# v of quarters 2 to 4 of a gMLP layer by seven half-size block products, with combined weights made beforehand

## The chip, the cores and the metric

The kernel runs on one core of a Trainium2 chip. The metric is the device time of one execution in microseconds (us). Engines are called as in the profile: PE (TensorE matmul), PEld (its weight load), DVE (VectorE), ACT (ScalarE), POOL (GpSimd) and SP (the engine that issues the DMAs here).

## The reference, cut to what matters

A trunk of two layers over 2048 tokens of width 1024, all in float32. Layer A is a chunked gMLP: it projects the normed and modulated input h to u, v and z (2048 columns each), mixes v over the tokens of a chunk of 128, and multiplies:

```
h = rms_norm(x, norm_g) * (1 + scale) + shift
u, v, z = jnp.split(h @ w_in, 3, axis=-1)
u = jax.nn.gelu(u)
v = rms_norm(jax.nn.gelu(v), sgu_g)
...
mixed = jnp.einsum('gts,bcsge->bctge', w_causal, v) + b_s.T[None, None, :, :, None]
y = u * mixed.reshape(bsz, s, A_WIDTH) * jax.nn.silu(z)
return x + gate * (y @ w_out)
```

Layer B projects keys and values once (`w_kv`), projects q (24 heads of 128) and a gate z from a second norm, and attends in three groups of heads: group 0 over neighbouring tokens, group 1 with dilation 4, group 2 with dilation 16. The three outputs are weighted by their softmax sums, gated and projected.

## The kernel before

**Precision.** Every float32 operand of a large product is split into a high part and a rest (`split`, L244: ACT copies the high part to the fp32r type, DVE subtracts it, L247). A product is then three matmuls of 128x512: high by high, high by low, low by high (`mm3`, L273).

**Quarters.** The work goes over the tokens in four quarters of 512 (Q = 0 to 3 in the code, quarters 1 to 4 here). In each quarter `layer_A` (L700) computes v (four blocks of 512 columns, `dense`, L277), then u and z (eight blocks each, `dense_f`, L299), then the output product (pd_o, `dense` again). `proj_B` (L793) follows with the key and value blocks (pd_kv), three q blocks (groups 2, 1, 0) and the gate block z (pd_z0b to pd_z3b). The last part, `finish` (L1105), makes the output of layer B.

`dense` loads 8 weight units of 128x512 for a block of columns, and runs them over the four token tiles in two pairs; one quarter's v is 4 x 8 x 4 x 3 = 384 matmuls and 32 weight units. The evacuation of v (`v_evac`, L559) is a Gelu from PSUM into the tile m and a square with its sum; m has two tiles of 128x4x1024. Then m is scaled (L711), and `mix` (L714) multiplies it with the chunk weights during u.

**Seven products.** The q and z blocks of layer B use `dense_s` (L376): a block of 512 tokens x 1024 x 1024 is cut into halves in each direction, and seven half-size products replace eight. Each is 4 k x 2 token tiles x 3 = 24 matmuls and 4 weight units. They go on two pairs of PSUM tiles, x and y; DVE adds partial results (`add`, L400). This needs sums of operands (`make_ops`, L491, names s1 to s4) and four combined weights t1 to t4 per block, which are made once: `combine_weights` (L320) loads the quarters of the weights, makes four subtractions of 128x512 on POOL (L344 to L347), and stores them to a DRAM tensor wt. It does so for four blocks in the first quarter, with `xin` tiles and `st` tiles in turn. The operands lie in four "big" tiles in the order 11, 12, 22, s1, s2, s3, s4 (`new_ops`, L460); "big" has six buffers of 16 KB per partition, and m takes two that these leave.

**Beside the stream.** Work for other engines and small pieces for PE are written as generators ("fillers"). `tick` (L84) is called after every few matmuls and runs `rate[0]` x its part steps of them. In quarter 1 the fillers are the modulation vectors and the combined weights; in layer A of quarters 2 to 4 they are the attention of the quarter before (`attend_local`, L1058: 80 steps, in quarter 3 with 8 more steps of `ada_gate`, each with two DVE instructions on L175 or L177); during the last blocks of `proj_B` they are the input of the next quarter (`make_hA`, L534: norm, transposes on PE, high part on ACT, low part on POOL, L456). What is left when `layer_A` returns is run at once (`drain`). The rate in layer A of quarters 2 to 4 is 1.5, so 24 steps fall into v, 24 into u, 24 into z and the rest into the output product. An attention step has its keys and values in an `xin` tile (`att_kv`, L906), makes scores on PE (L969 to L975), adds the bias on DVE (L978), takes exponentials on ACT (L988) and, in the form with `wrap`, three products and a select on POOL (L996 to L999, L1023).

**What sets the order.** Each engine has one queue and takes its instructions in order. That order is made by a planner before the run: it goes through the program with estimated durations and gives each engine, among the instructions that it takes for ready, the one that the program issues first. Buffers come from pools in turn (weights "w": 8 units, "raw" loads: 6, "xin": 4, "st" sum tiles: 8, "big": 6), and a tile waits until the last use of its buffer is over. `tc.issue_after` puts instructions behind a given one on its engine. All DMAs of the kernel are issued by SP.

Line 1260 and what follows is the loop over the quarters; `side_work` (L1245) is what quarter 1 has in the fillers.

## Time and profile before

| | us |
|---|---|
| median of 3 runs | 3000.92 (2997.74 to 3002.16) |
| the profiled execution, first to last instruction | 2998.7 |
| PE busy in it | 2951.4 |
| v of quarters 2, 3, 4 | 104.48, 106.04, 113.21 |
| output product of quarter 1 | 88.96 |
| one q block of quarter 2 | 38.08 |

The lengths of stages are the distances between the first matmuls of neighbouring stages in the trace, on the pd_ tiles of their names. The busy time of an engine in a stretch is the time in which at least one of its instructions runs; the mean of a group of matmuls is the time of one, and neighbours overlap. Idle time of an engine that is not the bottleneck costs nothing.

### The profile page before, as it was taken

To read this page: it belongs to the slowest core of one execution; us is meant where nothing else is said; L and a number is where in the kernel's file an instruction comes from. 1 tells how busy PE (TensorE), PEld (TensorE's weight loads), DVE (VectorE), ACT (ScalarE), POOL (GpSimd) and SP (SyncE) were. 2 spreads that over 40 slices of the span, in tenths; PEclk is the share of its full clock that TensorE was granted. 3 is DMA by queue.
4 is the path that set the end of the run, shared out by engine and by line. 5 is a ranking of instruction groups with operands and counts; after the bars stand their busy time and mean duration, and the time that the engine had idled before them with its cause. 6 is when DMAs were issued, how large, how long until landed. Compare 5 with 4: busy or idle time off the path is not lost.

```text
span 2998.7 us, 45113 instructions
## 1 busy us (share of the span) xinstructions
PE 2951.4 (98%) x14896; PEld 2473.5 (82%) x14896; DVE 1990.4 (66%) x3594; ACT 1625.1 (54%) x3308; POOL 744.4 (25%) x1044
## 2 busy tenths in 40 slices
PE   7999999999999999999999999999999999999999
PEld 5888888888888888888888888888888888977887
DVE  6868466764467376856567576856576576878772
ACT  4323355667366265756365366665465457866540
POOL 1057002410023013513123114323132020122322
PEclk9999999999999999999999999999999999999999
DMA  8899456763433366853433466833333366788642
GB/s 279 281 305 345 156 161 196 250 207 122 143 107 102 118 198 211 271 187 117 134 104 108 129 201 223 278 109 119 125 112 102 120 215 203 229 281 282 222 165 91
DMA packets 343677, 547.80 MB, mean 183 GB/s; under 512 B 36266, under 2 KB 135820, under 8 KB 343444
## 3 DMA queue, kind: packets, MB, share of 16 engines
q1 hardware_dynamic: 343444, 544.93, 56.4%
q8 instruction: 118, 1.93, 0.3%
q14 instruction: 115, 0.94, 0.1%
HBM read 439.28 MB, written 105.52 MB: 182 GB/s over the span
## 4 chain that ended last, share of the span: by engine, by line
PE 88%; DVE 3%; DMA 3%; issue 3%; POOL 2%; ACT 1%; SPq 0%; POOLq 0%; DVEq 0%; ACTq 0%
PE pd_o L275 11%; PE pd_v L275 10%; PE pd_kv L275 7%; PE pd_z L315 4%; PE pd_z L313 4%; PE pd_z L314 4%; PE pd_u L313 4%; PE po L1049 4%; PE pd_u L315 4%; PE pd_u L314 4%; PE pm L718 2%; PE pq L937 1%; PE pf L1227 1%; PE pf L1229 1%; PE pf L1228 1%
## 5 line engine op out<-in xcount | busy, mean ns | idle before, releaser
L275 PE MATMUL pd_o<-w_o,yh 128*128 128x512 f32 x1024 | 318.2, 391 | 0.0
L275 PE MATMUL pd_v<-w_v,hAh 128*128 128x512 f32 x960 | 303.5, 397 | 0.0
L275 PE MATMUL pd_kv<-w_kv,hkh 128*128 128x512 f32 x768 | 239.2, 393 | 0.3
L275 PEld LDWEIGHTS pd_o<-w_o,yh 128*128 128x128 f32 x1024 | 191.0, 188 | 39.1
L988 ACT ACTIVATE pr<-pr,stat,rt 128x256 f32<-128x256 f32 (+1 forms) x320 | 177.5, 556 | 62.7 <-DVE stat L982 36.8
L275 PEld LDWEIGHTS pd_v<-w_v,hAh 128*128 128x128 f32 x960 | 175.0, 188 | 37.8 <-issue 3.5
L313 PE MATMUL pd_u<-hAh,w_u 128*128 128x512 f32 x512 | 205.9, 402 | 0.0
L313 PE MATMUL pd_z<-hAh,w_z 128*128 128x512 f32 x512 | 204.6, 400 | 0.0
L315 PE MATMUL pd_z<-hAh,w_z 128*128 128x512 f32 x512 | 200.5, 392 | 0.0
L315 PE MATMUL pd_u<-hAh,w_u 128*128 128x512 f32 x512 | 200.2, 391 | 0.0
L275 PE MATMUL pd_o<-w_o,yl 128*128 128x512 f32 x512 | 200.0, 391 | 0.0
L314 PE MATMUL pd_z<-hAl,w_z 128*128 128x512 f32 x512 | 199.7, 390 | 0.0
L314 PE MATMUL pd_u<-hAl,w_u 128*128 128x512 f32 x512 | 199.7, 390 | 0.0
L275 PE MATMUL pd_v<-w_v,hAl 128*128 128x512 f32 x480 | 188.3, 392 | 0.0
L246 ACT ACTIVATE w_o<-raw_o 128x512 fp32r<-128x512 f32 x128 | 80.0, 630 | 184.6 <-PE pd_o L275 122.4
L246 ACT ACTIVATE w_u<-raw_u 128x512 fp32r<-128x512 f32 x128 | 78.7, 630 | 174.7 <-PE pd_u L315 78.3
L275 PEld LDWEIGHTS pd_kv<-w_kv,hkh 128*128 128x128 f32 x768 | 143.2, 189 | 30.6 <-ACT hkh L482 2.0
L247 DVE TENSOR_TENSOR w_o<-raw_o,w_o 128x512 fp32r<-128x512 f32 x128 | 91.9, 722 | 111.9 <-ACT w_o L246 111.4
L246 ACT ACTIVATE w_z<-raw_z 128x512 fp32r<-128x512 f32 x128 | 78.2, 627 | 160.9 <-PE pd_z L315 57.2
L996 POOL TENSOR_TENSOR dg<-pr,ident 128x256 f32<-128x256 f32 x76 | 60.5, 797 | 380.9 <-ACT pr L988 366.2
L1049 PEld LDWEIGHTS po<-kv,pT 128*128 128x128 f32 x1200 | 147.4, 192 | 8.5 <-ACT pT L899 2.1
L978 DVE SCALAR_TENSOR_TENSOR pr<-dist,rt,ps 128x256 f32<-128x256 f32 (+1 forms) x320 | 122.8, 431 | 43.0 <-PE ps L975 29.0
(664 smaller groups left out, 7680.8 us busy)
## 6 DMA issues: line engine op xcount, KB each, us to landing
raw_q<-in_b_w_in_dram SPq DMA_DIRECT2D x144, 256.0 KB, 3.4
raw_u<-in_a_w_in_dram SPq DMA_DIRECT2D x128, 256.0 KB, 3.6
raw_z<-in_a_w_in_dram SPq DMA_DIRECT2D x128, 256.0 KB, 3.2
raw_o<-in_a_w_out_dram SPq DMA_DIRECT2D x128, 256.0 KB, 3.0
raw_v<-in_a_w_in_dram SPq DMA_DIRECT2D x120, 256.0 KB, 4.1
qt<-qd SPq DMA_DIRECT2D x96, 260.0 KB, 2.9
raw_kv<-in_w_kv_dram SPq DMA_DIRECT2D x96, 256.0 KB, 2.9
od<-ot SPq DMA_DIRECT2D x96, 256.0 KB, 3.2
```

Source lines behind the costliest of these rows:

```text
L246: nc.scalar.activation(hi, src, AF.Copy)
L247: nc.vector.tensor_tensor(lo, src, hi.bitcast(F32), ALU.subtract)
L275: last_mm[0] = nc.tensor.matmul(pt, a, u[:, w, :], start=f, stop=e, skip_group_check=more)
L313: nc.tensor.matmul(pts[i], wh, hh[:, k, :], start=k == 0, stop=False)
L314: nc.tensor.matmul(pts[i], wh, hl[:, k, :], start=False, stop=False)
L315: nc.tensor.matmul(pts[i], wl, hh[:, k, :], start=False, stop=k == KT - 1)
L718: nc.tensor.matmul(pm[:, t * P:(t + 1) * P], m[e // 8][:, t, (e % 8) * P:(e % 8 + 1) * P], wst[:, e // 2, :], start=True, stop=True)
L937: nc.tensor.transpose(pq[:, h * P:(h + 1) * P], u["qt"][:, h * P:(h + 1) * P], ident)
L978: nc.vector.scalar_tensor_tensor(pr[:, i, :], dist[:, 256 - w:256], u["rt"][:, h:h + 1], psc[:, i, :], ALU.mult, ALU.add)
L988: nc.scalar.activation(pr[:, i, :], pr[:, i, :], AF.Exp, bias=mneg[:, i:i + 1], scale=u["rt"][:, h:h + 1], accum_out=lsum[:, i:i + 1])
L996: nc.gpsimd.tensor_tensor(dg, prev, ident.unsqueeze(1).broadcast_to([P, hp, P]), ALU.mult)
L1049: nc.tensor.matmul(po[:, h * P:(h + 1) * P], u["pT"][h // hp][:, h % hp, j, :], u["kv"][:, j, kh, 1, :], start=j == 0, stop=j == nk - 1)
```

## The change

Seven things are changed.

1. v of quarters 2 to 4 goes through `dense_s` in two blocks of 1024 columns (b = 4, 5), 2 x 7 x 24 = 336 matmuls and 56 weight units; quarter 1 keeps `dense`.
2. `sums_A` makes the operands out of hA: POOL adds high and low part into m[1] (four additions of 128x1024), DVE makes s1 to s4 in place, and each is split into two more big tiles. The DVE and ACT part is issued after the first product of the first block.
3. In the first of the two blocks `dense_s` has an order of its own (`late`): 11, 12 x 21, 22 x t4, then s2, s3, s1, s4, with 12 adds on DVE and 4 copies on ACT. The second block has the order that q and z have: 11, s2, 12, s3, s1, 22, s4, with 10 adds and 2 copies.
4. In these blocks the low half of every fourth weight unit is made by POOL (`shared`).
5. The combined weights of the two blocks are made in the output product of quarter 1, with `st` tiles alone, at rate 2.2 (before: rate 0).
6. Attention runs at rate 1.0 in v and 1.5 after it (1.6 in quarter 3): 16 steps in v, 24 in u, 24 in z, the rest in the output product. There its keys and values take a "w" buffer.
7. The operands of layer B lie in the order 11, 12, s2, s3, 22, s1, s4.

```diff
-    def split(hi, lo, src):
+    def split(hi, lo, src, e=None):
         nc.scalar.activation(hi, src, AF.Copy)
-        nc.vector.tensor_tensor(lo, src, hi.bitcast(F32), ALU.subtract)
+        (e or nc.vector).tensor_tensor(lo, src, hi.bitcast(F32), ALU.subtract)
...
-            split(u[:, 0, :], u[:, 1, :], raw)
+            split(u[:, 0, :], u[:, 1, :], raw, nc.gpsimd if shared and kk == nk - 1 else None)
...
+    def block_of(b):
+        return (b_w_in, b * D) if b < 4 else (a_w_in, AW + (b - 4) * D)
+
+    def combine_weights(blocks, where):
...
-                if i % 2:
+                if where == "sums" or where == "both" and i % 2:
...
+        if late:
+            product(x, "11", "11", True)
+            u2 = tmp("u")
+            for i in range(2):
+                nc.scalar.activation(u2[i][:, 0:512], x[i], AF.Copy)
+            late()
+            product(x, "12", "21", False)
+            for i in range(2):
+                evac(i, x[i], 0)
+            product(y, "22", "t4", True)
+            c21 = tmp("w")
+            for i in range(2):
+                nc.scalar.activation(c21[i][:, 0:512], y[i], AF.Copy)
+            product(x, "s2", "t2", True)
+            add(u2, x, u2)
+            product(y, "s3", "t3", True)
+            u3 = tmp("v")
+            add(u3, y, u2)
+            add(c21, [t[:, 0:512] for t in u3], c21)
+            for i in range(2):
+                evac(i + 2, c21[i], 0)
+            product(x, "s1", "t1", True)
+            add(u3, x, u3)
+            for i in range(2):
+                evac(i + 2, u3[i], 1)
+            add(u2, x, u2)
+            product(y, "s4", "22", True)
+            add(u2, y, u2)
+            for i in range(2):
+                evac(i, u2[i], 1)
+            return
...
-                for i, n in enumerate(("11", "12", "22", "s1", "s2", "s3", "s4"))}
+                for i, n in enumerate(("11", "12", "s2", "s3", "22", "s1", "s4"))}
...
+    def sums_A(Q, hA, m):
...
+        for n in ("11", "21", "22", "12"):
+            k, c = part[n]
+            hi, lo = (h[:, k:k + 4, c:c + 256].bitcast(F32) for h in hA)
+            nc.gpsimd.tensor_tensor(f[n], hi, lo, ALU.add)
+        s = {"s1": f["22"], "s3": f["21"], "s2": f["11"], "s4": f["12"]}
+
+        def sums():
+            nc.vector.tensor_tensor(s["s1"], f["21"], f["22"], ALU.add)
+            nc.vector.tensor_tensor(s["s3"], f["11"], f["21"], ALU.subtract)
+            nc.vector.tensor_tensor(s["s2"], s["s1"], f["11"], ALU.subtract)
+            nc.vector.tensor_tensor(s["s4"], f["12"], s["s2"], ALU.subtract)
+            for n in ("s2", "s3", "s1", "s4"):
+                split(*ops[n], s[n])
+        return ops, sums
...
     def layer_A(Q, hA, m, sqv, j0):
-        for j in range(j0, 4):
+        if Q:
+            ops, sums = sums_A(Q, hA, m)
+            for b in range(2):
+                ev = [v_evac(Q, m, sqv, 2 * b + n) for n in range(2)]
+                dense_s(ops, 4 + b, f"v{Q}{b}", lambda t, src, n: ev[n](t, src[:, 0:512]), None if b else sums, True)
+            rate[0] = 1.6 if Q == 2 else 1.5
+        for j in range(j0, 0 if Q else 4):
...
+        aside[0] = True
         if Q == 0:
-            rate[0] = 0
+            fillers.append(combine_weights((4, 5), "sums"))
+            rate[0] = 2.2
...
-        kv = xp.tile([P, 2, 512], F32, tag="xin", name=f"kv{g}_{b}")
+        pool, tag = (wp, "w") if aside[0] else (xp, "xin")
+        kv = pool.tile([P, 2, 512], F32, tag=tag, name=f"kv{g}_{b}")
...
-            rate[0] = 1.5
+            rate[0] = 1.0
         hk, hb, keep, rest = layer_A(Q, hA, m, sqv, 1 if Q == 0 else 0)
```

More of the change, by code (lines that the diff above doesn't have):

```diff
@@ L65, in trunk @@
     gd = dp.tile([2, D], F32, name="gd")
-    wt = [[dp.tile([512, 512], F32, name=f"wt{b}_{i}") for i in range(4)] for b in range(4)]
+    wt = [[dp.tile([512, 512], F32, name=f"wt{b}_{i}") for i in range(4)] for b in range(6)]
     fillers = []
@@ L318, in dense_f @@
             evac(i, pts[i])
-    def combine_weights():
-        todo = [(b, k) for b in (2, 1, 0, 3) for k in range(4)]
+    def block_of(b):
+        return (b_w_in, b * D) if b < 4 else (a_w_in, AW + (b - 4) * D)
+    def combine_weights(blocks, where):
+        todo = [(b, k) for b in blocks for k in range(4)]
         quads = {}
@@ L374, in sum_tile, with dense_s @@
         return tp.tile([P, 520], F32, tag="st", name=f"st_{nm}")
-    def dense_s(ops, b, nm, evac):
+    def dense_s(ops, b, nm, evac, late=None, shared=False):
         x, y = ([pst(f"pd_{nm}{c}{i}", "d") for i in range(2)] for c in "ab")
@@ L382, in dense_s @@
         flip[0] = not flip[0]
-        n0 = b * D
-        src = {"11": (b_w_in, 0, n0), "21": (b_w_in, 4, n0), "22": (b_w_in, 4, n0 + 512)}
+        w, n0 = block_of(b)
+        src = {"11": (w, 0, n0), "21": (w, 4, n0), "22": (w, 4, n0 + 512)}
         src.update({f"t{i + 1}": (wt[b][i], 0, 0) for i in range(4)})
         def product(pts, a, w, first):
-            us = wunits(*src[w], f"{nm}{w}_", 4)
+            us = wunits(*src[w], f"{nm}{w}_", 4, shared=shared)
             store_late(5)
@@ L557, in make_hA @@
                 yield
+    def sums_A(Q, hA, m):
+        t = [big.tile([P, 2, 2, 4, 256], F32R, tag="big", name=f"sA{Q}{i}") for i in range(2)]
+        ops = {n: (t[i // 2][:, i % 2, 0], t[i // 2][:, i % 2, 1]) for i, n in enumerate(("s2", "s3", "s1", "s4"))}
+        part = {"11": (0, 0), "12": (4, 0), "21": (0, 256), "22": (4, 256)}
+        f = {}
+        for i, (n, (k, c)) in enumerate(part.items()):
+            hi, lo = (h[:, k:k + 4, c:c + 256] for h in hA)
+            if n != "21":
+                ops[n] = hi, lo
+            f[n] = m[1][:, i, :].rearrange("p (k t) -> p k t", k=4)
+        for n in ("11", "21", "22", "12"):
[11 more added lines that the diff above has]
+        return ops, sums
     def v_evac(Q, m, sqv, j):
@@ L1246, in side_work @@
         yield from delayed(rest_of_ada())
-        yield from combine_weights()
+        yield from combine_weights((2, 1, 0, 3), "both")
     hA, m, sqv, ends = begin(affa)
@@ L1262, in trunk @@
             drain()
+        aside[0] = False
         nxt = {}
```

10 lines of the change are left out of this document (6 added, 4 removed).

## The prediction

> **What bounds the kernel now.** I read the page's span and busy lines first, then the chain of work that ended last, then the groups of matmuls, then one piece of the chain and the busy time by stage. Columns of a group: how many, total us, mean ns.
>
> ```profile
> span 2998.7 us, 45113 instructions
> PE 2951.4 (98%) x14896; PEld 2473.5 (82%) x14896; DVE 1990.4 (66%) x3594; ACT 1625.1 (54%) x3308; POOL 744.4 (25%) x1044
> ...
> PE 88%; DVE 3%; DMA 3%; issue 3%; POOL 2%; ACT 1%; SPq 0%; POOLq 0%; DVEq 0%; ACTq 0%
> ...
> L275 PE MATMUL pd_v<-w_v,hAh 128*128 128x512 f32 x960 | 303.5, 397 | 0.0
> L275 PE MATMUL pd_v<-w_v,hAl 128*128 128x512 f32 x480 | 188.3, 392 | 0.0
> ```
>
> TensorE is busy 98% of the span and is 88% of the chain, so a matmul that goes is worth its place in the stream. The mean of 397 ns is not that place: matmuls overlap. The chain in a q block, which already uses seven products, gives it:
>
> ```profile
> 1102.43 5.44 PE pd_q12a L275 x24
> 1107.87 5.44 PE pd_q12b L275 x24
> ...
> 1135.07 5.44 PE pd_q12a L275 x24
> 1140.51 0.68 PE pd_kv L275 x3
> ```
>
> Seven products of 24 matmuls take 1140.51 - 1102.43 = 38.08 us without a gap: 226.7 ns a matmul. Now the stages that matter (columns: stretch, length, then busy us and count of PE, PEld, DVE, ACT, POOL, granted clock, DMA share, GB/s). In order: z and output of quarter 1, v of quarter 2, a q block and the z block of quarter 2, v of quarters 3 and 4, a q block of quarter 4 with attention beside it.
>
> ```profile
> 234.43:321.56 87.13, 87.13 (x387) 72.18 (x386) 62.25 (x60) 37.95 (x65) 49.19 (x32) 1.00 0.99 336
> 321.56:410.52 88.96, 88.96 (x402) 73.68 (x401) 39.62 (x65) 27.36 (x53) 2.40 (x4) 1.00 0.37 114
> 634.89:739.37 104.48, 104.48 (x533) 87.90 (x532) 41.99 (x92) 71.16 (x150) 1.50 (x4) 1.00 0.38 122
> 1102.27:1140.35 38.08, 38.08 (x170) 31.54 (x168) 28.24 (x47) 23.85 (x41) 12.51 (x26) 1.00 0.70 205
> 1239.24:1280.24 41.00, 41.00 (x193) 33.89 (x192) 36.57 (x54) 27.44 (x46) 17.20 (x22) 1.00 0.88 289
> 1280.24:1386.28 106.04, 106.04 (x529) 87.66 (x528) 62.23 (x117) 60.31 (x126) 23.17 (x34) 1.00 0.48 154
> 1943.63:2056.84 113.21, 113.21 (x606) 96.49 (x605) 60.00 (x124) 71.68 (x149) 32.25 (x50) 1.00 0.36 117
> 2508.63:2601.48 92.85, 91.49 (x633) 82.09 (x632) 77.27 (x200) 79.21 (x229) 12.11 (x28) 1.00 0.74 226
> ```
>
> PE is full in all three v stages at clock 1.00. Vector and scalar engine have room there: 42 to 62 us and 60 to 72 us of 104 to 113. Everything below asks whether that room is enough.
>
> **What goes.** v of one quarter is 4 token tiles x 8 k x 4 blocks x 3 = 384 matmuls (1440 in the two groups = 288 in quarter 1 + 3 x 384). By seven products it is 2 x 168 = 336. So 3 x 48 = 144 matmuls go: 144 x 226.7 ns = **-32.6 us**. Nothing is added on PE. The attention steps are only placed elsewhere: 16 instead of 24 of them beside v, 8 more beside the output stage, where DVE is at 39.62 of 88.96.
>
> **How long the new v stage is on PE.** Attention takes what is left of a stage after 384 x 0.2267 = 87.1 us: 17.4, 19.0 and 26.1 us for 24 steps. With 16 steps it is about 11.6 in quarter 2 and 17.4 in quarter 4; in quarter 3 eight of the 16 are gate steps, so about 9.5. With 336 x 0.2267 = 76.2: 87.8, 85.7 and 93.6 us.
>
> **What the other engines must do in that time.** The prices (DVE splits by stretch, then groups of quarter 2, of quarter 3, of quarter 4 and of the whole run):
>
> ```profile
> 234.43:321.56 87.13, 32.86 (x33) 1.00 0.99 336
> 634.89:739.37 104.48, 21.21 (x33) 1.00 0.38 122
> 1102.27:1140.35 38.08, 18.86 (x29) 1.00 0.70 205
> 1280.24:1386.28 106.04, 22.86 (x33) 1.00 0.48 154
> 1943.63:2056.84 113.21, 20.51 (x29) 1.00 0.36 117
> ...
> L402 DVE TENSOR_TENSOR st_z0bu<-pd_z0bb,st_z0bu 128x512 f32<-128x512 f32 x2 | 1.3, 682 | 0.0
> L246 ACT ACTIVATE w_v<-raw_v 128x512 fp32r<-128x512 f32 x25 | 15.1, 628 | 9.7 <-PE pd_v L275 9.0 <-PE pd_z0bb L275 0.7
> L564 ACT ACTIVATE jk<-m 128x512 f32<-128x512 f32 x14 | 8.7, 628 | 0.1
> L562 ACT ACTIVATE m<-pd_v 128x512 f32<-128x512 f32 x14 | 7.9, 594 | 11.6 <-PE pd_v L275 11.4
> ...
> L177 DVE SCALAR_TENSOR_TENSOR acc_gb<-aw_gb,sc,acc_gb 128x512 f32<-128x512 f32 x14 | 10.4, 746 | 1.5 <-DMA aw_gb<-in_b_ada_w_dram 1.3
> ...
> L711 DVE TENSOR_SCALAR m<-m,rv 128x1024 f32<-128x1024 f32 x4 | 2.8, 752 | 3.8 <-POOL rv L241 3.8
> ...
> L1164 DVE TENSOR_TENSOR og<-og,og 128x1024 f32<-128x1024 f32 x16 | 20.8, 1302 | 1.6 <-ACT og L1162 1.3 <-DVE og L1100 0.2
> L1165 POOL TENSOR_TENSOR og<-og,zt 128x1024 f32<-128x1024 f32 x16 | 39.0, 2440 | 100.6 <-DVE og L1164 66.5 <-DMA zt<-zd 15.1 <-PE pf L1229 6.7
> L456 POOL TENSOR_TENSOR hAl<-h_a,hAh 128x512 fp32r<-128x512 f32 x24 | 31.9, 1329 | 52.8 <-ACT hAh L454 52.8
> ```
>
> DVE, new, per quarter: 56 weight units instead of 32, of which every fourth gives its low half to POOL, so 42 x 0.65 (18.86 / 29) = 27.3; 22 adds (12 in the first block, 10 in the second) at 0.68 = 15.0; 4 sums and 4 low halves of 128x1024 at 1.30 = 10.4; scaling m 2.8. That is 55.5. Attention's part of the old stage (all, less splits, less m; in quarter 3 less 16 gate steps' instructions at 0.746) is 18.0, 24.5 and 36.7, of which 16 steps keep 12.0, 24.2 (half of it, and the gate's 12) and 24.5. Sums: **67.5 of 87.8, 79.7 of 85.7, 80.0 of 93.6 us**. ACT in quarter 2: 71.16 less 32 x 0.628, less 16 x (0.594 + 0.628) = 19.6 for Gelu and squares, leaves 31.4 for attention; 2/3 of it, 56 x 0.628, about 9 for four high halves of double size and six copies, and 19.6 give 84 of 87.8. All fit, closely. That a stage can run so is shown above: the z block had DVE 36.57 of 41.00 and PE 41.00; the q block of quarter 4 had ACT 79.21 of 92.85 and PE 91.49.
>
> **Where it will not be free: POOL and DVE in each other's way.** POOL gets 4 operand sums at 2.44 and 14 low halves at 1.33 = 28.4 us a quarter. Quarter 1, where the q weights are combined, shows what that does (POOL, then DVE):
>
> ```profile
> 237.42 1.83 POOL L346 TENSOR_TENSOR cw<-cw,cw 128x512 f32<-128x512 f32 x1
> 239.33 1.62 POOL L347 TENSOR_TENSOR cw<-cw 128x512 f32<-128x512 f32 x1
> ...
> 239.72 1.77 DVE L731 TENSOR_TENSOR mt<-mt,u 128x512 f32<-128x512 f32 x1
> ```
>
> The DVE product of two SBUF tiles started inside L347 and took 1.77 us, ending only after L347 had (240.95). On average, with POOL busy 49.19 of 87.13 us (56%), a split took 32.86 / 33 = 1.00 us against 0.65 in the q block: +0.35. Scaled by POOL's share in the new stages (28.4 of 87.8; with half of quarter 3's 23.17, 40 of 85.7; with two thirds of quarter 4's 32.25, 50 of 93.6) on some 50 such instructions, 66 with the gate's, DVE is held up 10, 19 and 17 us: 78, 99 and 97 against 87.8, 85.7 and 93.6. The excess of 13 and 3 us is the bound from above for a steady shortage. Against it stands the lead: eight weight buffers are two products, 10.9 us, that DVE can lose during the stage, and the evacuation at its end can run on into u. So I take 13 - 10.9 = 2 us in quarter 3 and nothing in quarter 4, where a price of 0.35 us is from the nearest row and could be half as much.
>
> The Trainium skill, SBUF — State Buffer, section "SBUF: two separate sides", says that VectorE with two SBUF inputs and a GpSimd instruction that reads SBUF share one port pair as an exclusive lock, held for a whole instruction. The row of 1.77 us agrees, and the rule speaks against moving work to POOL; taken at its word it is the second rival below.
>
> **The start of each v stage.** This is the densest place. Quarter 3 (POOL, then DVE, then the chain):
>
> ```profile
> 1273.18 1.30 POOL L456 TENSOR_TENSOR hAl<-h_a,hAh 128x512 fp32r<-128x512 f32 x1 [4.60 <-ACT hAh L454]
> ...
> 1272.35 0.68 DVE L247 TENSOR_TENSOR w_v<-raw_v,w_v 128x512 fp32r<-128x512 f32 x1
> 1280.40 1.28 DVE L402 TENSOR_TENSOR st_z1bu<-pd_z1bb,st_z1bu 128x512 f32<-128x512 f32 x2
> ...
> 1280.40 1.36 PE pd_v L275 x6
> ```
>
> hA is whole at 1274.5; its scratch, the tile of s2 and s3, is free since the fourth of seven z products. So POOL makes the four sums from 1274.5 to 1284.3, to 1287 if DVE breaks in four times. Behind them on POOL stands the fourth low half of the first product, 1.3 us, due at 1280.4 + 3 x 1.36 + 0.9 of attention = 1285.4: 0 to 3 us late. The DVE's 10.4 us of sums start with the third POOL sum, near 1282; before the fourth product (1280.4 + 16.3 + 3 attention steps = near 1300) DVE also owes nine low halves (5.9), three steps (4.6) and z's last adds (1.3): 1304 if nothing blocks, 1308 with POOL's lock, less the three or four halves that it did ahead. So the stage starts between 0 and 8 us late; I take **3 us in quarter 2** (its attention is half as costly), **7 in quarter 3** (5, and the 2 above) and **5 in quarter 4: +15 us**. Nothing waits in strict program order: L247 for v at 1272.35 ran before z's adds at 1280.40, which the program issues earlier, so the planner will put ready splits before sums that wait.
>
> **The output stage of quarter 1.** Eight combinations: 32 POOL subtractions (1.6 to 1.8 us by the rows of L346 and L347, some 55 of 89 us), 8.4 MB in and 8.4 MB out over 76 us, 221 GB/s on top of 114. That is what z of quarter 1 carried, 336 GB/s at a DMA share of 0.99, with PE 87.13 of 87.13. Its 30 steps, of 35 that the stage gives, end just before the norm asks for the same eight sum tiles; a late store there would cost one landing. Between 0 and 3 us; I take +1. The added chain at the end of v (two adds, 1.3 us, before the last Gelu) lies beside u's first 48 matmuls, 10.9 us: 0. Weight loads rise to 56 x 256 KB in 88 us, 167 GB/s, under the q block's 205: 0. The steps moved from v to later stages: 0, between -2 and +2.
>
> **Sum.** -32.6 + 15 + 1 = -16.6 us. The profiled execution's span becomes 2998.7 - 16.6 = 2982; the median of the runs, 3000.92, is 2.2 us above the span (their own spread is 4.4), so **2984 us**.
>
> **Rivals.** (1) The cover holds: the planner finds a place for the sums and DVE never falls behind. For it: the z and q blocks above, full on PE with DVE at 89% of the stretch. Against: they have no 10 us lump at their head. 3000.9 - 32.6 + 2 = 2970. (2) The lock decides: DVE is the bound of v in quarters 3 and 4, the excess of 13 and 3 us is not absorbed and comes on top of the lateness at the start (3, 5, 5): 29 us, 3000.9 - 32.6 + 29 + 1 = 2998. For it: +0.35 us a split in quarter 1. Against: the lead of two products, and that PE lost nothing there. (3) Slower: the fourth low half of each product stands on POOL behind an attention product that waits for its exponential.
>
> ```profile
> POOL dg L996 <- ACT pr L988: 366.2, 36, 57.9
> ```
>
> POOL stood 366 us before that instruction in the run. If a low half is queued behind one, PE waits for ACT's chain once a product. From 32.6 / 42 = 0.8 us a product on, the change loses; at 1.2 us it is 3000.9 - 32.6 + 50 + 1 = 3019. Against: the planner orders POOL by estimated readiness, and the estimate has to be wrong by microseconds. That the matmuls do not go is no rival: their number is written in the loops.
>
> **How the numbers follow.** Forecast 0.58 (2975 to 2994), rival 1 0.24, rival 2 0.11, rival 3 0.07. Range: from just under rival 1 (2968) to 2997, which leaves out rival 3, half of rival 2 and the tail of rival 1. About 0.2% (6 us) can be told from no change: faster 0.83, same 0.10, slower 0.07.
>
> **What would show it.** Right: pd_v with 288 + 3 x 336 = 1296 matmuls; v stages of 90 to 95, 90 to 95 and 96 to 102 us; PE idle in their first 25 us, with DVE or POOL named as releaser; L247 longer than 0.69 us beside POOL's sums. Rival 1: 88, 86 and 94 us. Rival 2: DVE over 95% in v of quarters 3 and 4, PE idle spread over the stage. Rival 3: PE released by POOL L247 in every product. Wrong altogether: PE idle in the output stage of quarter 1, or u and z stages longer by more than the attention that they take over.

## The result: slower, 3020.03 us against 3000.56

The median of 4 runs is 3020.03 us (3019.13 to 3021.16); the kernel before, in 4 runs beside it, 3000.56 (2997.74 to 3002.16). The ratio is 1.0066 [1.0052, 1.0081]. The forecast was 2984, the range ended at 2997, and the sign is wrong. The profiled execution has a span of 3018.5 us, 19.8 above that of before. Its page, and the view of the cores:

```profile
span 3018.5 us, 45519 instructions
PE 2937.2 (97%) x14752; PEld 2453.0 (81%) x14752; DVE 2125.0 (70%) x3714; ACT 1664.4 (55%) x3397; POOL 904.3 (30%) x1130
```
```profile
core 0: 3018.5 us, clock 0.994
```

The 144 matmuls are gone (14896 to 14752), and the span is longer all the same. PE's busy time fell by 14.2 us only, less than half of what 144 matmuls take, and its idle time rose from 47.3 to 81.3 us. The mean granted clock was 0.998 before: (1 - 0.994) x 3018.5 = 18 us of lost clock against 6, so half speed can account for up to about 12 us of the difference.

The busy time by stage (columns as in the prediction): the output stage of quarter 1, the z blocks ahead of the three v stages, then the v stages of quarters 2, 3 and 4.

```profile
323.58:420.50 96.92, 91.82 (x402) 75.48 (x400) 54.61 (x65) 27.17 (x53) 46.85 (x35) 0.96 0.81 276
604.35:648.20 43.85, 41.26 (x189) 33.17 (x188) 42.72 (x53) 21.69 (x39) 25.89 (x25) 1.00 0.76 246
1247.35:1291.84 44.49, 41.38 (x194) 33.59 (x192) 38.97 (x49) 23.68 (x41) 32.49 (x28) 1.00 0.78 255
1923.84:1967.33 43.49, 41.25 (x189) 33.17 (x188) 42.36 (x51) 22.91 (x40) 24.43 (x23) 1.00 0.79 261
648.20:741.54 93.34, 90.12 (x434) 74.47 (x435) 66.46 (x110) 80.62 (x166) 21.77 (x14) 0.98 0.62 198
1291.84:1390.88 99.04, 92.10 (x407) 73.68 (x408) 77.59 (x122) 70.35 (x137) 39.78 (x28) 0.95 0.67 220
1967.33:2066.55 99.22, 96.00 (x481) 80.44 (x481) 81.30 (x137) 82.31 (x165) 45.07 (x45) 0.98 0.61 192
```

In each of these stages PE now stands idle for 2.2 to 6.9 us, and four have a clock under 1.00. From the distances between stages, against before and against the forecast:

| | before | after | change | forecast | missed by |
|---|---|---|---|---|---|
| v of quarters 2, 3, 4 | 323.7 | 291.6 | -32.1 | -41.6 | 9.5 |
| u, z, output of quarters 2 to 4 | 973.9 | 1008.9 | +35.0 | +24.0 | 11.0 |
| z blocks before the v stages | 122.2 | 131.8 | +9.7 | 0 | 9.7 |
| output stage of quarter 1 | 88.95 | 96.91 | +8.0 | +1 | 7.0 |
| all else | | | -0.8 | 0 | -0.8 |
| span | 2998.7 | 3018.5 | +19.8 | -16.6 | 36.4 |

(Forecast of v: 90.8, 92.7 and 98.6 us. The 24.0 us are attention that the forecast itself moved out of v, 5.8, 9.5 and 8.7, and called free.) Four misses of about the same size, and all to one side.

**Where PE stood in the output stage of quarter 1.** The waits of PE in that stage, and the order of time (POOL, then DVE):

```profile
PE pd_o L275 <- DVE w_o L247: 5.1, 1, 5.1
```
```profile
324.54 1.62 POOL L351 TENSOR_TENSOR st_cw<-st_cw,st_cw 128x512 f32<-128x512 f32 x1
326.25 1.62 POOL L352 TENSOR_TENSOR st_cw<-st_cw,st_cw 128x512 f32<-128x512 f32 x1
...
323.56 9.96 DVE L815 TENSOR_TENSOR yl<-mt,yh 128x512 fp32r<-128x512 f32 x6 [0.58 <-PE pd_z L314]
333.44 3.42 DVE L812 TENSOR_TENSOR mt<-mt,z 128x512 f32<-128x512 f32 x2
336.79 1.75 DVE L247 TENSOR_TENSOR w_o<-raw_o,w_o 128x512 fp32r<-128x512 f32 x1
```

Six low halves of y take 9.96 us, 1.66 each: each one waits for one POOL subtraction, and each subtraction for one of them. The split that PE needs stands behind them and comes at 338.5.

**Where PE stood before the v stages.** The order of time at the end of the z block of quarter 2, just ahead of v of quarter 3 (POOL, DVE, PE):

```profile
1272.62 2.72 POOL L610 TENSOR_TENSOR m<-hAh,hAl 128x1024 f32<-128x1024 f32 x1
1285.45 2.72 POOL L610 TENSOR_TENSOR m<-hAh,hAl 128x1024 f32<-128x1024 f32 x1
1288.14 1.26 POOL L247 TENSOR_TENSOR w_v<-raw_v,w_v 128x512 fp32r<-128x512 f32 x1
...
1269.48 6.40 DVE L247 TENSOR_TENSOR w_z1bt<-raw_z1bt,w_z1bt 128x512 fp32r<-128x512 f32 x3 [0.92 <-ACT w_z1bt L246]
1288.20 2.28 DVE L614 TENSOR_TENSOR m<-m 128x1024 f32<-128x1024 f32 x1 [2.29 <-POOL m L610]
1290.41 0.68 DVE L247 TENSOR_TENSOR w_v<-raw_v,w_v 128x512 fp32r<-128x512 f32 x1
1291.01 1.27 DVE L407 TENSOR_TENSOR st_z1bw<-pd_z1ba,st_z1bu 128x512 f32<-128x512 f32 x2
...
1291.84 0.70 PE L275 MATMUL pd_v20a<-w_v,hAh 128*128 128x512 f32 x2 [3.11 <-DVE st_z1bw L407]
```

Two things are seen. The additions of high and low part lie inside the z block, where three weight splits beside them take 6.40 us, 2.13 each. And DVE, in its fixed order, has a sum (L614) ahead of z's last adds (L407): it stands 2.29 us for the last POOL addition, and PE, which needs the adds' PSUM tiles, 3.11. Ahead of v of quarters 2 and 4 DVE did not wait for POOL there, but two sums (L614, L615) still stood ahead of z's last adds, and PE waited 1.3 us each time. The POOL additions themselves were early: the last one ended at 1288.2, 3.7 us before the first matmul of v, where the forecast had them end 4 to 7 us after it.

**Where PE stood inside the first v blocks.** The longest wait of quarter 2 and the longest of quarter 3 after the block's start, then ACT in order of time in quarter 2:

```profile
PE ps L1043 <- ACT qT L1014: 1.9, 1, 1.9
PE pd_v20a L275 <- ACT st_v20u L413: 1.6, 1, 1.6
```
```profile
651.06 2.94 ACT L246 ACTIVATE sA<-m 128x1024 fp32r<-128x1024 f32 x3
...
656.50 0.67 ACT L1014 ACTIVATE qT<-pq,gqk 128x512 f32<-128x512 f32 x1
```

PE idles 3.2, 3.7 and 3.2 us in these blocks. The releaser of the longest wait is ACT, in quarter 4 too (2.4 us for qT): the high halves of the sums (sA), which come as late as DVE's sums, stand in ACT's queue ahead of the copies and the attention steps that PE needs next, as the rows of quarter 2 show. Without the sums (kernel 14) these waits are gone. The prediction named DVE or POOL as releaser.

**And the clock.** The stretch after the idle before v of quarter 3, the stretch after the idle in the output stage, then two neighbouring stretches in the second block of v of quarter 3:

```profile
1293.10:1296.50 3.40, 3.40 (x10) 2.63 (x9) 3.40 (x4) 3.18 (x5) 0.00 (x0) 0.50 0.98 270
337.30:344.10 6.80, 5.51 (x13) 4.34 (x14) 4.60 (x3) 0.59 (x2) 3.89 (x3) 0.50 0.68 245
1374.98:1378.39 3.41, 1.43 (x7) 0.91 (x6) 3.37 (x7) 2.36 (x4) 1.82 (x1) 1.00 0.98 356
1378.39:1381.81 3.42, 3.42 (x10) 2.65 (x9) 3.25 (x7) 2.05 (x4) 0.76 (x1) 0.50 0.82 271
```

After the idle of 3.11 us come 3.4 us at half clock, after that of 5.10 us 6.8, and after one of 1.98 us 3.4 again. At half clock a matmul starts every 427 ns instead of every 226.7, so 8 start where 15 would fit, and one such stretch costs about 1.6 us. In all there are nine, 34 us; before there were three, 10.2 us (without the piece at the very end of each span).

The length of one idle does not decide. The half-clock stretches of a profile all start on one grid of slots of 3.41 us. Over the slots of all nineteen profiles, without the first 100 and the last 30 us of each: each of the 71 full-clock slots with 2.0 us of idle or more was followed by a slot at half clock, and none of the 4407 with under 1.4 us was; of the 112 between, 44 were. So it is the idle time that falls into one slot, in sum. Kernel 1 below shows the other side.

### The profile page after: what moved, and what is told of

The parts are those of the page before. It is cut to its first block, busy times and chain, and to the rows that moved or that the text cites. A ratio compares the mean times of both kernels' runs of the same rounds, so it can differ in the third digit from the quotient of the medians.

```text
span 3018.5 us, 45519 instructions
## 1 busy us (share of the span) xinstructions
PE 2937.2 (97%) x14752; PEld 2453.0 (81%) x14752; DVE 2125.0 (70%) x3714; ACT 1664.4 (55%) x3397; POOL 904.3 (30%) x1130
## 5 line engine op out<-in xcount | busy, mean ns | idle before, releaser
L246 ACT ACTIVATE w_z<-raw_z 128x512 fp32r<-128x512 f32 x128 | 79.2, 628 | 173.4 <-PE pd_z L315 64.2
L246 ACT ACTIVATE w_u<-raw_u 128x512 fp32r<-128x512 f32 x128 | 79.0, 629 | 160.9 <-PE pd_u L315 74.9
L246 ACT ACTIVATE w_o<-raw_o 128x512 fp32r<-128x512 f32 x128 | 79.2, 628 | 144.9 <-PE pd_o L275 66.2
L247 DVE TENSOR_TENSOR w_z<-raw_z,w_z 128x512 fp32r<-128x512 f32 x128 | 100.9, 797 | 78.0 <-ACT w_z L246 77.6
L1123 PE MATMUL po<-kv,pT 128*128 128x128 f32 x1200 | 149.7, 275 | 1.0 <-ACT pT L970 1.0
L275 PE MATMUL pd_kv<-w_kv,hkl 128*128 128x512 f32 x384 | 149.6, 391 | 0.0
L247 DVE TENSOR_TENSOR w_o<-raw_o,w_o 128x512 fp32r<-128x512 f32 x128 | 100.9, 799 | 68.2 <-ACT w_o L246 68.1
```

The source lines that it names most:

```text
L246: nc.scalar.activation(hi, src, AF.Copy)
L247: (e or nc.vector).tensor_tensor(lo, src, hi.bitcast(F32), ALU.subtract)
L275: last_mm[0] = nc.tensor.matmul(pt, a, u[:, w, :], start=f, stop=e, skip_group_check=more)
L1123: nc.tensor.matmul(po[:, h * P:(h + 1) * P], u["pT"][h // hp][:, h % hp, j, :], u["kv"][:, j, kh, 1, :], start=j == 0, stop=j == nk - 1)
```

## The experiments

My theory after the result: the sums and the combined weights cost through POOL's and DVE's mutual hold and the order on DVE, each cost locally, at a point where PE has no lead. The rivals: the pace of attention is the loss; the DMA traffic of the combined weights is; the seven products themselves do not give 32.6 us. Each kernel is the changed one with the edit shown, or another kernel named. Ratios are to the kernel before, run beside each series, with the 95% interval in brackets; its median was 2998.1 to 3000.6 us, so that kernels of different series are better compared by ratio. Stage lengths are those of each kernel's one profiled execution. Line numbers differ from kernel to kernel.

**1. The four additions on DVE.**

```diff
-            nc.gpsimd.tensor_tensor(f[n], hi, lo, ALU.add)
+            nc.vector.tensor_tensor(f[n], hi, lo, ALU.add)
```

> The changed kernel (3020 us), with the four additions of high and low part per quarter on DVE instead of POOL. Theory 'lock': POOL's 128x1024 additions, which the planner put into the z block before v, hold up every DVE instruction with two SBUF inputs, and PE waits for the weights; without them the z blocks fall from 43.9, 44.5, 43.5 to about 41 us (-9), the idle 3.1 us at the start of v of quarter 3 goes, and the half-clock windows after it: 3000 to 3010 us. Theory 'DVE load': v is short of DVE time, and 4 x 1.2 = 5 us more of it a quarter make it longer: 3020 to 3035 us.

Measured: 3003.80, 1.0012 [1.0003, 1.0022], as the first theory expected: some 16 us of the 19.5 came back, 9.8 of them in the z blocks and 4.9 in v. The z blocks:

```profile
601.27:641.80 40.53, 40.53 (x189) 33.49 (x188) 38.24 (x56) 24.13 (x43) 16.49 (x20) 1.00 0.81 268
1239.35:1280.35 41.00, 41.00 (x193) 33.88 (x192) 36.62 (x55) 25.70 (x44) 24.46 (x24) 1.00 0.84 278
1911.64:1952.18 40.54, 40.54 (x190) 33.50 (x188) 38.26 (x56) 25.31 (x44) 16.53 (x20) 1.00 0.86 285
```

PE is full again in each. In the first and third DVE was busy 42.72 and 42.36 us before the edit, and 38.24 and 38.26 after it with three and five instructions more in the stretch. So work taken *onto* DVE shortened DVE's time there: it was the hold, not the amount.

Inside the first v block of quarter 3 this kernel has one idle of 3.44 us (for ACT w_v20t L246), longer than the 3.11 us above, and no half clock after it: it falls about evenly into two slots of the clock's grid.

```profile
1285.22:1288.64 3.42, 1.62 (x9) 1.03 (x7) 3.42 (x4) 3.38 (x5) 1.26 (x1) 1.00 0.62 190
1288.64:1292.05 3.41, 1.76 (x8) 1.50 (x9) 3.41 (x5) 3.41 (x8) 0.00 (x0) 1.00 0.86 311
1292.05:1295.46 3.41, 2.41 (x12) 1.67 (x11) 3.41 (x5) 2.52 (x4) 1.65 (x1) 1.00 0.00 1
```

**2. All low halves on DVE.**

```diff
-                dense_s(..., None if b else sums, True)
+                dense_s(..., None if b else sums, False)
```

> The changed kernel, with every low half of a weight unit on DVE (no fourth one on POOL). Theory 'lock': 14 POOL instructions of 1.3 us a quarter go and 14 of 0.65 us come to DVE; v shortens by 1 to 3 us a quarter, 3011 to 3017 us. Theory 'DVE load': DVE has 9 us more a quarter, v gets longer by 2 to 5 us each, 3026 to 3035 us. The third rival of the prediction (low halves behind attention on POOL): -10 us or more, 3010 us or less.

Measured: 3010.50, 1.0034 [1.0021, 1.0047], 9.5 us better, between the two ranges for a gain. But by stage 4.8 of it lie in the output stage of quarter 1, which the edit does not touch (another order there), and 6.8 in v of quarter 3; v of quarters 2 and 4 got 1 us longer each. Low halves on POOL did hurt once, in quarter 3's second block, and not per product.

**3. Combining alone:** the kernel before with the combined weights made in the output stage of quarter 1 and never used. The order of layer B's operands and the place of keys and values are those of the change; kernel 4 has them too, without the combining, and its stage has 88.95 us.

```diff
         if Q == 0:
-            rate[0] = 0
+            fillers.append(combine_weights((4, 5), "sums"))
+            rate[0] = 2.2
```

> The kernel before with the combining of the two v blocks in the output stage of quarter 1 and nothing that uses it: v by dense products, attention at 1.5. Theory 'lock': the output stage of quarter 1 takes 96.9 us as in the changed kernel instead of 88.96, all other stages are as before: 3008 to 3010 us. Rival, that the stage got longer by something else that comes with the change (operand order, buffers): 3000 us, output stage 89 us.

Measured: 3006.62, 1.0025 [1.0015, 1.0034]; the stage has 95.22 us (before 88.96), the six low halves of y 9.46:

```profile
323.36:418.58 95.22, 90.62 (x402) 74.62 (x400) 55.39 (x65) 27.18 (x53) 47.47 (x35) 0.98 0.80 277
```
```profile
323.33 9.46 DVE L815 TENSOR_TENSOR yl<-mt,yh 128x512 fp32r<-128x512 f32 x6 [0.74 <-PE pd_z L314]
```

**4. Pace alone:** the changed kernel with v by `dense` in all quarters and without the combined weights; pace, place of the keys and order of the operands as changed.

```diff
-        if Q:
+        if False:
             ops, sums = sums_A(Q, hA, m)
...
-        for j in range(j0, 0 if Q else 4):
+        for j in range(j0, 4):
...
```

> The kernel before with the new pace of attention alone (1.0 in v, then 1.5, in quarter 3 1.6), the buffers for keys and values and the operand order of the change; v by dense products, nothing combined. If the pace costs by itself: u, z and output of quarter 3 lose the 8 us (and those of quarter 4 the 4 us) by which they grew beyond the attention that they took over: 3008 to 3013 us. If it does not: 2998 to 3003 us.

Measured: 3003.11, 1.0012 [1.0003, 1.0022], just above the lower of the two ranges. v got 5.9, 9.8 and 9.1 us shorter, u, z and output together 6.0, 13.0 and 10.4 longer: free in quarter 2, +3.2 in quarter 3 and +1.4 in quarter 4.

**5. Both edits of 1 and 2.**

> The changed kernel with both: high and low part added on DVE, and every low half of a weight unit on DVE. Theory 'lock' (POOL's reading instructions cost DVE more than they save it): z blocks at 41 us, v of quarter 3 as in the run with all low halves on DVE (92 us) or shorter, 2993 to 3000 us. Theory 'DVE load' (each piece was better off on POOL once the other is on DVE): 3004 to 3012 us.

Measured: 3000.96, 1.0008 [0.9999, 1.0017]: POOL makes no operand of v any more, and the time is that of before, a little above the range of the first theory.

**6. The subtractions of the combined weights on DVE too** (kernel 5 with it).

```diff
+            e = nc.vector if where == "sums" else nc.gpsimd
-            nc.gpsimd.tensor_tensor(t1, t3, t1, ALU.subtract)
+            e.tensor_tensor(t1, t3, t1, ALU.subtract)
...
```

> The run before in this list (both on DVE), and the four subtractions of the combining in the output stage of quarter 1 on DVE as well: 32 x 0.65 = 21 us more DVE time in a stage where DVE had 40 of 89 us before the change. Theory 'lock': the output stage of quarter 1 falls from 92 to 97 us to 89 to 91, 2987 to 2996 us. Rival, that the stage is long by the DMA traffic of the combining: it stays at 92 to 97, 2993 to 3000 us.

Measured: 2998.51, 1.0002 [0.9992, 1.0011], a miss: the stage has 95.42 us still. DVE in its order of time:

```profile
329.29 0.68 DVE L353 TENSOR_TENSOR st_cw<-st_cw,st_cw 128x512 f32<-128x512 f32 x1
...
331.82 3.69 DVE L816 TENSOR_TENSOR yl<-mt,yh 128x512 fp32r<-128x512 f32 x6
335.43 1.29 DVE L813 TENSOR_TENSOR mt<-mt,z 128x512 f32<-128x512 f32 x2
336.63 0.69 DVE L247 TENSOR_TENSOR w_o<-raw_o,w_o 128x512 fp32r<-128x512 f32 x1
```

The hold is gone (six in 3.69, not 9.96), and now the subtractions themselves stand in front: the eighth split comes at 336.6, where it came at 336.8. PE waits 4.7 us for it, where it waited 5.1. The same point of the stage, another reason.

**7. The gate steps in quarter 2** instead of quarter 3 (kernel 6 with it).

```diff
-            if Q == 2:
+            if Q == 1:
                 fillers.append(ada_gate...
-            rate[0] = 1.6 if Q == 2 else 1.5
+            rate[0] = 1.6 if Q == 1 else 1.5
```

> The run with all three on DVE, and the gate's fillers (16 DVE instructions with two SBUF inputs, 0.75 us each, and their loads) in quarter 2 instead of quarter 3, with the pace 1.6 there. If v of quarter 3 is long because DVE is full: layer A of quarter 3 falls by 5 to 9 us, that of quarter 2 rises by 2 to 4, in all -3 to -5 us against the run with all three on DVE. If the cause in quarter 3 is the attention itself: within 2 us of it.

Measured: 2998.07, 1.0000 [0.9991, 1.0010]. Layer A of quarter 3 lost 8.2 us and quarter 2's gained 5.8, most of it in its output stage, where steps were left over; the 3 to 5 us expected in all did not come.

**8. Combining that only writes** (kernel 3 with it): three fills of each sum tile instead of each subtraction; same DMAs.

```diff
+            if where == "sums":
+                for t in (t1, t3, t2, t4):
+                    for _ in range(3):
+                        nc.gpsimd.memset(t, 0.0)
+                return
```

> As the run with the combining alone (v by dense products, nothing uses the combined weights), but POOL only writes: each of the four subtractions is replaced by three fills of the same tile with zeros, so the loads, the stores and a busy POOL stay and its reads of SBUF go; the combined weights of v are not computed. Theory 'lock by reads': the output stage of quarter 1 takes 89 us (2999 us). Rival 'DMA traffic' or 'any busy POOL': 94 to 97 us, as with the subtractions (3006 us).

Measured: 3000.36, 1.0007 [0.9998, 1.0017]. The stage, the six low halves, and POOL beside them:

```profile
321.88:410.83 88.95, 88.95 (x402) 73.67 (x400) 39.17 (x65) 27.02 (x53) 46.04 (x97) 1.00 0.88 304
```
```profile
321.85 3.70 DVE L820 TENSOR_TENSOR yl<-mt,yh 128x512 fp32r<-128x512 f32 x6 [0.81 <-PE pd_z L314]
319.99 14.23 POOL L352 MEMSET st_cw<- 128x512 f32 x30 [21.27 <-DMA st_cw<-in_a_w_in_dram]
```

POOL is as busy as in kernel 3 (46.04 against 47.47), the DMAs are the same, their share is higher, and PE is full. So neither traffic nor a busy POOL costs the 6 us. What the fills lack is that POOL *reads*; each is also shorter, 0.47 us against some 1.6. The Trainium skill, SBUF — State Buffer, section "Who interferes with whom", says that a VectorE instruction with two SBUF inputs contends with a GpSimd instruction that reads SBUF and not with one that only writes; 9.46 against 3.70 us agrees.

**9. A light start** (kernel 7 with it): attention at rate 0.25 in the first v block and 1.5 in the second, then 2.0 in u (2.3 in quarter 2) and 1.5 from z on.

> The run with all three on DVE and the gate in quarter 2 (2998 us), with attention's pace at 0.25 in the first of the two blocks of v, 1.5 in the second, 2.0 in u (2.3 in quarter 2) and 1.5 after it. If the idle time left in v (4.1, 7.8, 4.6 us in the first blocks, under 1 in the second) comes from DVE and ACT having sums, splits and attention at once: it falls to 0 to 2 a block, and the output stages lose their waits on late attention (6.9 us in quarter 2): 2982 to 2991 us. If it comes from the chain of the sums alone: idle time stays, 2995 to 3000 us.

Measured: 2998.31, 1.0000 [0.9990, 1.0009]. v has 85.2, 93.7 and 100.2 us (kernel 7: 87.0, 100.6 and 97.4), but u of quarters 3 and 4 128.9 and 134.1 (121.6 and 121.7). Their output stages are 4.5 and 4.7 us shorter, which does not make up for it. Attention that leaves the start of v is paid in u, and the gain of 7 to 16 us hoped for did not come. The output stage of quarter 1, whose code is that of kernels 6 and 7, has 88.95 us here, 91.24 in kernel 7 and 95.42 in kernel 6: with the subtractions on DVE the order alone decides whether combining is free.

**10. Combining later in the stage** (kernel 7 with it): six steps' delay, rate 2.6.

> The run with all three on DVE and the gate in quarter 2, with the combining begun six steps later in the output stage of quarter 1, at rate 2.6, when the low halves of y that end layer A's z are done. If the stage is long because both meet at its start: 89 to 90 us in place of 91 to 95, 2993 to 2997 us. If any 21 us of DVE work there cost it: no change, 2997 to 3000 us.

Measured: 3018.74, 1.0069 [1.0054, 1.0084]; a miss of 20 us. The waits between 380 and 400 us, and SP's order:

```profile
ACT w_o L246 <- DMA raw_o<-in_a_w_out_dram: 23.3, 2, 22.9
...
PE pd_o L275 <- ACT w_o L246: 9.1, 1, 9.1
```
```profile
380.18 2.58 SPq L359 DMA_DIRECT2D wt<-st_cw  x4
385.44 2.20 SPq L338 DMA_DIRECT2D st_cw<-in_a_w_in_dram  x4
387.69 2.50 SPq L359 DMA_DIRECT2D wt<-st_cw  x4
390.29 7.93 SPq L254 DMA_DIRECT2D raw_o<-in_a_w_out_dram  x8
```

SP issues all DMAs in one order. Stores that wait for a sum stand ahead of eight weight loads; PE pays 9.1 us. The stage has 100.09 us, 8.9 more than in kernel 7. Another 10.4 us lie in v, which the edit does not touch, and 6 in stages of the rest of the kernel; this profile has 54.6 us at half clock against 17.1 in kernel 7, and why they are there was not followed.

**11 and 12. Kernels 9 and 10 together, and the same with combining on POOL.**

> Both of these edits (light start of v, late combining): the sum of the two, 2978 to 2989 us. If they only move waits on: 2993 to 3000 us.

> The run with both edits, with the combining's subtractions on POOL again as in the change. Theory 'lock': the splits of the output weights meet POOL's subtractions (1.6 us each instead of 0.7), but without the low halves of y beside them; the output stage takes 90 to 94 us, 1 to 5 us more than in the run with both. If the place alone counted: within 1 us of it.

Measured: 3007.17, 1.0035 [1.0021, 1.0048], and 3011.72, 1.0046 [1.0029, 1.0063]; the output stage of quarter 1 has 97.85 and 103.29 us. Kernel 11 misses both of its ranges, and kernel 12's stage its 90 to 94 us. With POOL the stage is 5.4 us longer than with DVE.

**13. No combining** (kernel 5 with it): t1 to t4 are plain quarters of the weights, so v of quarters 2 to 4 is not computed; loads, splits, matmuls and adds are all there.

```diff
-            fillers.append(combine_weights((4, 5), "sums"))
-            rate[0] = 2.2
+            rate[0] = 0
...
-        src.update({f"t{i + 1}": (wt[b][i], 0, 0) for i in range(4)})
+        src.update({f"t{i + 1}": (wt[b][i], 0, 0) if b < 4 else (w, 4 * (i // 2), n0 + 512 * (i % 2)) for i in range(4)})
```

> The run with operand sums and low halves on DVE (3001 us), without the combining of the two v blocks: the products take plain quarters of the weights in place of the combined ones, so v of quarters 2 to 4 is not computed, but loads, splits, matmuls and adds are all there. The output stage of quarter 1 goes back to 88.95 us and nothing else changes: 2992 to 2996 us. If the combining costs more than its own stage (late stores, loads of combined weights): below 2990 us.

Measured: 3007.98, 1.0033 [1.0019, 1.0047]; a miss. The output stage of quarter 1 has its 88.95 us again, but v is 1.8, 2.5 and 3.9 us longer than in kernel 5, and u, z and output together 3.8. Why is not settled; the order on DVE and SP at v's start is another one.

**14. The products alone** (kernel 13 with it): no sums; the places of s1 to s4 are taken by 22, 12, 11 and 12.

> The run before in this list, without the operand sums as well: the products take halves of the input that exist, so neither sums nor combined weights are made (v of quarters 2 to 4 is not computed); 336 matmuls, 56 units and all adds stay. Theory 'lump at the start': the idle time in the first blocks of v (4.8, 9.2, 4.5 us) is the sums' and falls to under 1.5 each: 2976 to 2984 us. Rival, splits, adds and attention fill DVE and ACT by themselves: idle time stays above 3 each, 2988 to 2995 us. Full cover, the 32.6 us of matmuls less the 4 us that the pace cost alone: 2970 us.

Measured: 2981.43, 0.9939 [0.9924, 0.9954]. As expected if the idle time is the sums'. The first v block of quarter 3 in kernel 13 and in this one, then this one's of quarter 4:

```profile
1275.30:1329.12 53.82, 47.34 (x210) 38.13 (x208) 47.18 (x80) 39.58 (x72) 6.24 (x8) 0.94 0.62 199
```
```profile
1271.07:1312.70 41.63, 41.63 (x198) 34.52 (x197) 35.64 (x62) 32.44 (x63) 6.67 (x8) 1.00 0.77 251
1927.08:1973.45 46.37, 46.37 (x238) 39.05 (x237) 34.79 (x66) 38.05 (x77) 11.15 (x14) 1.00 0.56 180
```

Without the sums PE is full from the first matmul; the two kernels differ by nothing else, and by 26.6 us in the median, 24.4 in the three v stages. Its v stages have 88.48, 85.63 and 93.49 us against 98.57, 96.29 and 104.12 in kernel 4, which has the dense products: 31.4 us less. In v the seven products do give what they should. The whole kernel is only 21.7 us below kernel 4 in the median: of the difference between their profiles, u, z and output take 5.4 us back, and stages that neither edit touches 6.6.

**15. Kernel 9 without combining.**

> The run with the light start of v (2998 us), without the combining (plain quarters of the weights, v of quarters 2 to 4 not computed): what seven products with real operand sums would bring if the weights came for nothing. If the combining's stage is what varies from run to run: 2985 to 2992 us, and a narrower spread of runs. If the rest varies as well: 2990 to 2998 us.

Measured: 3001.57, 1.0006 [0.9997, 1.0016], a miss like kernel 13's: no gain from leaving the combining out, and the reason is open as there.

**16. The sums spread and later** (kernel 7 with it): the four additions after the first product, the sums and splits after the third; the second block's product 11, which needs no sum, is drawn ahead of s2; attention at 0.5 in the first block, 1.5 in the second.

```diff
             product(x, "11", "11", True)
-            late()
+            late(0)
             product(x, "12", "21", False)
...
             product(y, "22", "t4", True)
+            late(1)
+            product(y, "11", (w1, 0, n1), True)
             product(x, "s2", "t2", True)
...
```

> The run with all three on DVE and the gate in quarter 2 (2998 us), with the operand sums issued in two parts (high and low part added after the first product, the four sums and splits only after the third), the first product of the second block drawn ahead of the product with s2 (one product, 5.44 us, more before the sums are needed), and attention at 0.5 in the first block and 1.5 in the second. Theory 'lump at the start': idle time in the first blocks of v (4.1, 7.8, 4.6 us) falls to 1 to 3 each: 2984 to 2992 us, below the kernel before. If the sums cost their 10 us of DVE wherever they stand: 2994 to 3000 us.

Measured: 2992.10 (2987.24 to 2997.48, 12 runs), 0.9973 [0.9964, 0.9981]: faster than both kernels. Its v stages:

```profile
635.62:720.52 84.90, 83.48 (x388) 68.17 (x387) 74.99 (x126) 70.88 (x139) 0.00 (x0) 1.00 0.76 245
1276.30:1375.34 99.04, 95.17 (x478) 79.74 (x477) 80.69 (x143) 79.55 (x155) 24.08 (x30) 0.98 0.58 185
1941.37:2038.86 97.49, 93.74 (x477) 78.39 (x476) 85.69 (x147) 80.01 (x155) 22.92 (x29) 1.00 0.63 199
```

They have 281.4 us together, against 291.6 in the changed kernel and 285.0 in kernel 7, and PE idles 1.4, 3.9 and 3.8 us in them against 3.2, 6.9 and 3.2 in the changed kernel. So v is 3.6 us shorter than in kernel 7, by the spreading and the new pace in v together; the two were not separated. Of the other 6 us between their profiled executions 2.1 lie in u, z and output of quarters 2 to 4, 1.7 in the output stage of quarter 1 and 2.5 elsewhere, and the profiled execution is the fastest of its twelve.

**17. Kernel 16 with the gate steps in quarter 3,** 2.0 in u and 1.5 from z on.

> The same with the gate's fillers in quarter 3 as in the change, and attention at 2.0 in u and 1.5 after it. If the output stages' waits on late attention matter: 3 to 5 us below the run with the sums late, 2980 to 2989 us. If u pays for it (as in the run with the light start): level with it or above.

Measured: 2997.69, 0.9997 [0.9986, 1.0008]: above kernel 16, where 3 to 5 us below it was the hope. So 5.6 us of kernel 16's gain depend on where the gate steps are and on the pace.

## Why the prediction was wrong, step by step

**The matmuls that go: right in v.** -32.6 forecast, -31.4 by kernels 14 and 4. **The chain and its bound: right;** PE is the bound, and each place where it stands is paid in full.

**The start of the v stages: the mechanism right, the order and the size wrong.** This is the step that turned the sign: +15 us in the sum, 33.6 by the runs. The lump was named: four POOL sums, 10.4 us of DVE behind them, low halves in between. It failed at one sentence, "the planner will put ready splits before sums that wait". It did for the splits seen in the trace of before; for the sums, DVE stood at L614 for POOL in quarter 3 with z's adds behind it, and in quarters 2 and 4 ran two sums ahead of those adds. In v the high halves of the sums stood in ACT's queue in the same way, which the prediction counted in ACT's total only. The lateness of 15 us was forecast inside v, and the z blocks before it at nothing. Against kernel 14, the changed kernel has 4.9 + 13.4 + 5.7 = 24.0 us more in v and 9.6 in the z blocks, 33.6 us; the sums alone, on DVE, are worth 24.4 in v (kernels 13 and 14), and POOL's additions 9.8 in the z blocks (kernel 1). It eats all that the products give. The z blocks were shown in the prediction as proof that PE stays full with DVE at 89% of a stretch; the same row says that DVE had 4 us to spare there, and four POOL instructions of some 2.7 us, each holding up a DVE instruction or two, took more. (ACT's sum for quarter 2, 84 us, adds up to 85; nothing hangs on it.)

**POOL and DVE in each other's way: priced as a mean, paid at a point.** +0.35 us a split, taken over a whole stage, was meant as the price. Kernel 8 shows the cause to be right and the size wrong: with both queues full of two-input work each DVE instruction takes a POOL instruction's length, 1.66 us for 0.62, and that for nine in a row.

**The output stage of quarter 1: +1 forecast, +8 measured.** The cover was taken from z of quarter 1, where POOL's subtractions lengthen DVE's instructions as well, but PE waits for none of them. At the head of the output stage DVE owes the last splits of the first eight weights, and has six low halves of y and two products ahead of the one that PE waits for; there is no lead. The warning stood in the text as a sign of "wrong altogether", not in the sum.

**The steps moved to later stages: 0 forecast, +11.0 measured.** Kernel 4 shows 4.6 of it without the new v (3.2 + 1.4). Another 5.6 stand between kernel 4 and the changed kernel (1003.3 and 1008.9 us in these stages). They need neither the sums nor idle time of PE in v: kernel 14, where PE is full in v, has 1008.7 us too. What they come from is open.

**The clock: not in the sum.** Up to about 12 us of the loss are half clock after idles, inside the terms above. A slot with more than about 2 us of idle was worth 1.6 us on top. The Trainium skill, TensorE: Matmul & The Clock Gate, section "HAM oscillation — how this bites in real kernels", states as a rule no idle gaps of TensorE over about 3.4 us; here one of 1.98 us was followed by half clock and one of 3.44 us in kernel 1 was not, and the measurement decides.

**The rivals.** The second (the lock decides, 2998) had the right cause, and too little of it, since it counted v alone; its sign, DVE over 95% in v of quarters 3 and 4, did not come (78% and 82%). The third, low halves on POOL behind something that waits, was there at a small size: of the four waits of PE in the v stages put down to POOL L247 the longest is this, in the second block of quarter 3.

```profile
PE pd_v21a L275 <- POOL w_v21t L247: 1.2, 1, 1.2
```

**What stays open:** why kernels 13 and 15, with work left out, gained nothing. Also what u, z and output take beyond kernel 4. Small edits moved the planner's order by several us in stages that they do not touch, and executions of one kernel lie up to 14 us apart (kernel 17), so that differences under some 5 us between two of these kernels are not put down to their edits unless a row shows the place.

## What to carry to other kernels

A product scheme that saves matmuls moves work to the engines that prepare the operands, and the saving is kept only if that work has a lead: ask at each stage head which instruction the bound engine needs next, and what stands ahead of it in its producer's queue. Two-input elementwise work that is moved from VectorE to GpSimd can cost VectorE more than it saves: kernel 1 took the additions back and DVE's own time in the z block fell. Spread a lump over products that do not need it, as kernel 16 does, and time the pace of what runs beside it together with it.

## What the runs showed of the hardware beyond this

Fills on GpSimd leave VectorE alone (six two-input instructions in 3.70 us with POOL 52% busy), reads by GpSimd do not (9.46 us at 50%). Half clock came in pieces of 3.4 us, or 6.8 after the longest idle, on a fixed grid of 3.41 us: always after a slot with 2.0 us of idle or more in sum, never after a slot at full clock with under 1.4. So two short idles in one slot cost what a long one does, and one of 3.44 us across two slots cost nothing more than itself.
